# A decoder trunk in fp32: when weights are cast beside the copies and evacuations of a seven-product scheme

## The chip, the cores and the metric

The kernel runs on one core of a Trainium2 chip. The metric is the device time of one execution in microseconds (us); less is better. Engines are named as the profile names them: PE (TensorE, matmuls), PEld (its weight loads), DVE (VectorE), ACT (ScalarE), POOL (GpSimd, here mostly the issuer of accumulating DMAs) and SP (SyncE, the issuer of loads).

## What is computed

Two layers on a sequence of 512 tokens with 1024 features, everything in float32. Each layer adds half a SwiGLU feed-forward (FFN), a mixer, and half a second FFN; the mixer of layer 0 is a gated linear attention, that of layer 1 a stick-breaking attention. A final RMSNorm ends it. The FFN has 2816 inner columns:

```python
def swiglu(h, w_gate, w_up, w_down):
    return (jax.nn.silu(h @ w_gate) * (h @ w_up)) @ w_down
...
for i in range(DEPTH):          # DEPTH = 2
    x = x + 0.5 * swiglu(rmsnorm(x, ffn1_norm[i]), ffn1_w_gate[i], ffn1_w_up[i], ffn1_w_down[i])
    h = rmsnorm(x, mix_norm[i])
    y = gla_mixer(h, ...) if i % 2 == 0 else sb_mixer(h, ...)
    x = x + y
    x = x + 0.5 * swiglu(rmsnorm(x, ffn2_norm[i]), ffn2_w_gate[i], ffn2_w_up[i], ffn2_w_down[i])
return rmsnorm(x, final_norm)
```

So there are four FFNs, and the change concerns them alone.

## The kernel before

**Products.** Activations lie transposed, features on the 128 partitions, the 512 tokens along the row (T = 512, H = 256 is half of them). A float32 product is made of three fast ones: each weight tile is split into a high part, which ACT casts (`wh`, line 138 in `Entry.split`), and a low part, raw minus high, which DVE subtracts (`wl`, line 139). Activations are split in the same way (`hh`, `hl`, lines 816 and 817). Each logical matmul is then wh·h, wl·h and wh·l, so PE's order of work always needs two other engines a little ahead of it.

**Seven products for eight.** Lines 694 to 799 (`seven`) compute a chunk of 256 weight columns in a scheme of seven half-size products in place of eight. Beside the raw weights it needs sums of weight quarters, which DVE makes: `s12` (L704, L705) and `s34` (L710, L711), the "second sums". One chunk is two entries of the feed. The first, `body_1`, has three weight units (a11 of 128x512, s12 of 128x1024, a2 of 128x1024) and four products, in this order: into ps_w with a11; into ps_q with s12; again into ps_w with s12; into ps_z with a2. Between the first and the third ACT copies ps_w to ps_z (L746), since both sums begin with that product; the third adds to ps_w and so must wait for the copy. The second entry, `body_2`, has one unit (s34) and three products: into ps_w, ps_q, ps_w. Results are evacuated by ACT copies and silus and by DVE adds and gates (L729, L732, L765, L769), then closed, that is split into hh and hl. An FFN has 18 such chunks (9 gate, 9 up); the others go by plain products (`feat`).

**Down projection.** Six groups of one or two chunks (`GROUPS`) are projected back as soon as their activations are closed. Groups 1 and 3 go by the same scheme (`seven_down`, lines 354 to 450), in two parts each, so 4 pairs in each FFN and 16 in all. Here `body_1` makes two products b11 (one for each of two 128-column halves m = 0, 1) into ws[0] and ws[1], copies both to zs (L408), then makes t1 into ps_q, t2 on to ws and b21, with the first half of a2, on to zs; behind them come the DVE adds of ps_q, ps_w and ps_z into the residual x (`add`, L396). `body_2` makes t3 on to ws (so it needs s34's split and the add of ws done), b22 on to ps_q, and t4 on to ws with the second half of a2. The other groups' products are evacuated by DVE into x (L345) or, for the products named in `HOMES`, by ACT into a scratch tile that POOL adds to x with an accumulating DMA (L340, L341): one in each part of groups 0 and 2, three in each part of group 4.

**Feed.** `Feed.start` (lines 146 to 161) opens the next entry. Before that it splits, that is casts, this entry and up to two behind it, as long as their big units (128x1024) are not more than four, the number of buffers. Loads of raw weights are issued up to six entries ahead on SP's queue. Instructions go to each engine in an order that a scheduler makes from the order of the program and priorities; on the engine they then run in that order.

Of the kernel before, what the change touches and what calls it, by code (L numbers as in the profile page):

```python
# [10 lines left out]
F32 = mybir.dt.float32  # L11
F32R = mybir.dt.float32r
# [3 lines left out]
ALU = mybir.AluOpType  # L16
PSUM = bass.MemoryType.PSUM

P = 128
T = 512  # L20
# [26 lines left out]
def decoder(ctx: ExitStack, tc: tile.TileContext, a: dict, out: bass.AP):  # L47
    nc = tc.nc
# [5 lines left out]
    wp = ctx.enter_context(tc.tile_pool(name="wp", bufs=4))  # L54
# [53 lines left out]
    class Entry:  # L108
# [3 lines left out]

        def __init__(self, units, body):
            self.units, self.body, self.W, self.views = units, body, None, None

        def view(self):

# [1 line left out]
                self.views = [view(ch.load()) for ch, view, _, _ in self.units]  # L119
            return self.views  # L120

        def split(self):
            if self.W is None:
                self.W = []
                for r, (_, _, n, m) in zip(self.view(), self.units):
                    few = n * m < 1024
                    if few:

                        h, l = (
                            st["few"].tile([P, n * m], F32R, tag="v" + t, bufs=1, name="w" + t) for t in "hl"  # L130
                        )
                    else:
                        h, l = (wp.tile([P, n * m], F32R, tag="w" + t, bufs=4, name="w" + t) for t in "hl")
                    h, l = (t.rearrange("p (n m) -> p n m", m=m) for t in (h, l))
                    pieces = r if isinstance(r, tuple) else (r,)
                    for i, part in enumerate(pieces):
                        k = slice(i * n // len(pieces), (i + 1) * n // len(pieces))
                        st["cut"] = nc.scalar.copy(h[:, k], part).ins  # L138
                        nc.vector.tensor_tensor(out=l[:, k], in0=part, in1=h[:, k].bitcast(F32), op=ALU.subtract)  # L139
                    self.W.append((h, l))  # L140

    class Feed:
        def __init__(self):
# [210 lines left out]
    def seven_down(pool, w, r0, hs, part):  # L354
# [3 lines left out]
        H = T // 2  # L358
# [5 lines left out]
        v = {}  # L364
# [31 lines left out]
            nc.vector.scalar_tensor_tensor(out=x, in0=ps, scalar=0.5, in1=x, op0=ALU.mult, op1=ALU.add)  # L396

        def body_1(W):
            a11, s, v["a2"] = W
            ws, zs, qs = [], [], []  # L400
            for m in range(2):
                ws.append(psum("ps_w")[:, 0:H])
                prod(ws[m], a11, 0, m, "b11", True)
            for m in range(2):


                zs.append(psum("ps_z")[:, 0:H])
                nc.scalar.copy(zs[m], ws[m])  # L408
# [74 lines left out]
    st = {}  # L483
# [129 lines left out]
    class FFN:  # L613
# [12 lines left out]
        def __init__(self, wg, wu, wd, gi, nxt, first=False, last=False):  # L626
# [7 lines left out]
            for group, (c0, c1) in enumerate(self.GROUPS):  # L634
# [59 lines left out]
        def seven(self, ch, group=None):  # L694
# [31 lines left out]
            def gate(o, c, t):  # L726

                if group is None:
                    st["silu"] = nc.scalar.activation(pair(o[:, c : c + H]), t, AF.Silu).ins  # L729
                else:  # L730
                    g = self.gates[0 if o is v["o"][0] else 1]
                    nc.vector.tensor_tensor(  # L732
                        out=pair(o[:, c : c + H]), in0=t, in1=pair(g[:, c : c + H]), op=ALU.mult
                    )

            def body_1(W):


                a11, s, a2 = W
                v["a2"] = a2  # L740
                v["w"], v["q"] = psum("ps_w"), psum("ps_q")
                z = psum("ps_z")[:, 0:H]
                w, q = (v[n][:, 0:H] for n in "wq")
                o0, o1 = v["o"] = [self.tp.tile([P, T], F32, tag="t", name=n) for n in ("o0", "o1")]
                prod(w, a11, 0, half(0, 0))
                nc.scalar.copy(z, w)  # L746
# [5 lines left out]
                nc.scalar.copy(pair(o0[:, H:T]), flat(w))  # L752
                yield
                prod(z, a2, 0, half(4, 0), first=False)
                gate(o0, 0, flat(z))
                yield

            def body_2(W):
                (s,) = W
                w, q = (v[n][:, 0:H] for n in "wq")  # L760
                o0, o1 = v["o"]
                prod(w, s, 0, lambda j: self.t_half(2, j), first=False)
                u3 = self.tp.tile([P, H], F32, tag="c", bufs=1, name="u3")
                nc.scalar.copy(pair(u3), flat(w))
                nc.vector.tensor_tensor(out=o1[:, H:T], in0=u3, in1=o1[:, H:T], op=ALU.add)  # L765
                yield
                prod(q, s, 4, half(4, 1), first=False)
                oh = pair(o0[:, H:T])
                nc.vector.tensor_tensor(out=oh, in0=flat(q), in1=oh, op=ALU.add)  # L769
                gate(o0, H, oh)  # L770
                if group is not None:
                    close_0(o0)
                gate(o1, H, pair(o1[:, H:T]))
                yield
                prod(w, v["a2"], 0, lambda j: self.t_half(3, j), first=False, c0=P)
                gate(o1, 0, flat(w))
# [83 lines left out]
        def evac_u(self, ps, group):  # L860
            t = self.tp.tile([P, T], F32, tag="t", name="t")
            if not self.normed:
                nc.vector.tensor_tensor(out=pair(t), in0=flat(ps), in1=pair(st["R"]), op=ALU.mult)
            nc.vector.tensor_tensor(
                out=pair(t), in0=flat(ps) if self.normed else pair(t), in1=pair(self.gates.pop(0)), op=ALU.mult
            )
            self.close(t, group)

        def close(self, t, group):
            h = self.hp.tile([P, T], F32R, tag="hh", name="hh")  # L870
# [454 lines left out]
    class SB:  # L1325
# [588 lines left out]
```

## Time and profile before

| | us |
|---|---|
| median of 3 runs | 1779.91 (1779.62 to 1782.33) |
| the profiled execution | 1779.44 |
| its span (first to last instruction) | 1777.5 |
| PE busy in it | 1756.3 |
| DVE busy | 1508.6 |
| ACT busy | 1081.6 |
| mean granted clock of PE | 0.999 of full speed |

Times in the profile count from the start of the span. A row of a timeline holds the start, the duration, the engine, the line, the operation, the tiles (output, then inputs) and their shapes; two equal instructions in a row are one row with x2. A duration on ACT or DVE is longer than the distance to the next instruction, since neighbours overlap. A bracket at the end of a row is the idle time ahead of the instruction and what ended it. A row of the waits holds who waited for whom, the total, the number of times and the longest wait.

### The profile page before, as it was taken

The page shows a single profiled execution, that of the slowest core. Times are in us where ns is not written, and L with a number is a line of the kernel's source. Part 1 is how long each engine was busy: PE and PEld are TensorE (multiplying, and loading weights), DVE is VectorE, ACT ScalarE, POOL GpSimd, SP SyncE. Part 2 cuts the span into 40 slices and gives each one's busy share as a digit, 9 for nine tenths or more (in the row PEclk, how much of TensorE's full clock was granted, in tenths as well). Part 3 has the DMA queues.
Part 4 walks back from the last instruction along what each step waited for, and adds up shares of the span by engine and source line. Part 5 has one row for each costly group of instructions (what it writes and reads, how often), then busy time and mean ns, then how long its engine had stood idle before and what let it go on. Part 6 is the DMA issues. An engine that isn't in the chain of part 4 may idle for free.

```text
span 1777.5 us, 31388 instructions
## 1 busy us (share of the span) xinstructions
PE 1756.3 (99%) x12714; PEld 1630.4 (92%) x12714; DVE 1508.6 (85%) x2471; ACT 1081.6 (61%) x1886; POOL 58.4 (3%) x80
## 2 busy tenths in 40 slices
PE   9999999999999999999999999999999999999998
PEld 8999999889888899999889999999888888999997
DVE  8999797786888989888798988967898679997985
ACT  7556556554655556555565555555889745665655
POOL 0000000200000000000000000010000000000000
PEclk9999999999999999999999999999999999999999
DMA  5543435422123433344424344342212134434342
GB/s 168 153 120 118 125 103 148 112 72 72 49 95 95 130 108 119 119 119 126 141 85 130 103 124 135 110 120 83 84 49 78 66 95 131 131 108 129 114 131 65
DMA packets 186820, 193.93 MB, mean 109 GB/s; under 512 B 4978, under 2 KB 171172, under 8 KB 186676
## 3 DMA queue, kind: packets, MB, share of 16 engines
q1 hardware_dynamic: 177760, 175.91, 31.7%
q0 software_dynamic: 8672, 15.74, 4.9%
q8 instruction: 99, 1.62, 0.4%
q14 instruction: 45, 0.37, 0.1%
q10 hardware_dynamic: 244, 0.29, 0.0%
HBM read 175.17 MB, written 2.10 MB: 100 GB/s over the span
## 4 chain that ended last, share of the span: by engine, by line
PE 67%; DVE 22%; ACT 5%; DMA 3%; issue 3%; POOL 0%; DVEq 0%; SPq 0%; ACTq 0%; POOLq 0%
PE ps_w L719 16%; PE ps_d L80 11%; PE ps_q L719 8%; PE ps_f L80 7%; DVE wl L139 5%; PE ps_t L80 4%; PE ps_z L719 4%; PE ps_w L390 4%; PE ps_b L80 3%; PE ps_q L390 2%; ACT wh L138 2%; DMA raw<-in_ffn_w_gate_dram 1%; DVE ts L826 1%; PE ps_z L1402 1%; DVE nl L817 1%
## 5 line engine op out<-in xcount | busy, mean ns | idle before, releaser
L139 DVE TENSOR_TENSOR wl<-raw,wh 128x1024 fp32r<-128x1024 f32 x241 | 255.0, 1059 | 59.8 <-ACT wh L138 59.1
L138 ACT CAST wh<-raw 128x1024 fp32r<-128x1024 f32 x241 | 221.7, 921 | 77.1 <-PE ps_f L80 22.6
L139 DVE TENSOR_TENSOR wl<-s,wh 128x1024 fp32r<-128x1024 f32 x176 | 214.3, 1218 | 47.2 <-ACT wh L138 47.2
L719 PE MATMUL ps_w<-th,wh 128*128 128x256 f32 x864 | 239.4, 277 | 4.2 <-ACT ps_z L746 4.1
L719 PE MATMUL ps_w<-th,wl 128*128 128x256 f32 x864 | 237.6, 275 | 0.0
L719 PE MATMUL ps_w<-tl,wh 128*128 128x256 f32 x864 | 237.6, 275 | 0.0
L138 ACT CAST wh<-s 128x1024 fp32r<-128x1024 f32 x176 | 184.1, 1046 | 69.1 <-DVE s L705 19.3
L719 PEld LDWEIGHTS ps_w<-th,wh 128*128 128x128 f32 x864 | 165.8, 192 | 7.6 <-ACT ps_z L746 7.6
L80 PE MATMUL ps_f<-xh,wh 128*128 128x512 f32 x432 | 166.4, 386 | 0.0
L719 PEld LDWEIGHTS ps_w<-tl,wh 128*128 128x128 f32 x864 | 165.9, 192 | 0.0
L719 PEld LDWEIGHTS ps_w<-th,wl 128*128 128x128 f32 x864 | 165.8, 192 | 0.0
L80 PE MATMUL ps_f<-xh,wl 128*128 128x512 f32 x432 | 164.2, 380 | 0.5 <-DVE wl L139 0.5
L80 PE MATMUL ps_f<-xl,wh 128*128 128x512 f32 x432 | 163.9, 379 | 0.0
L80 PE MATMUL ps_d<-hl,wh 128*128 128x512 f32 x416 | 158.0, 380 | 1.7 <-DVE hl L817 1.7
L80 PE MATMUL ps_d<-hh,wh 128*128 128x512 f32 x416 | 158.0, 380 | 0.5 <-ACT hh L816 0.5
L80 PE MATMUL ps_d<-hh,wl 128*128 128x512 f32 x416 | 157.7, 379 | 0.0
L139 DVE TENSOR_TENSOR wl<-rawd,wh 128x1024 fp32r<-128x1024 f32 (+1 forms) x100 | 96.0, 963 | 16.0 <-ACT wh L138 15.8
L138 ACT CAST wh<-rawd 128x1024 fp32r<-128x1024 f32 (+1 forms) x100 | 82.8, 845 | 39.3 <-PE ps_d L80 25.6
L341 POOL DMA_DIRECT2D x<-d x56 | 48.6, 879 | 1531.1 <-ACT d L340 829.9
L80 PEld LDWEIGHTS ps_f<-xl,wh 128*128 128x128 f32 x432 | 81.6, 189 | 11.5
L80 PEld LDWEIGHTS ps_f<-xh,wl 128*128 128x128 f32 x432 | 81.7, 189 | 11.3 <-DVE wl L139 0.9
L80 PEld LDWEIGHTS ps_f<-xh,wh 128*128 128x128 f32 x432 | 81.7, 189 | 10.8
(355 smaller groups left out, 5324.9 us busy)
## 6 DMA issues: line engine op xcount, KB each, us to landing
raw<-in_ffn_w_gate_dram SPq DMA_DIRECT2D x43, 1024.0 KB, 5.5
raw<-in_ffn_w_up_dram SPq DMA_DIRECT2D x43, 1024.0 KB, 5.4
rawd<-in_ffn_w_down_dram SPq DMA_DIRECT2D x84, 512.0 KB, 3.7
x<-d POOLq DMA_DIRECT2D x56, 256.0 KB, 4.6
raw<-in_gla_w_in_dram SPq DMA_DIRECT2D x12, 1024.0 KB, 5.3
raw<-in_sb_w_in_dram SPq DMA_DIRECT2D x16, 512.0 KB, 3.8
raw<-in_gla_w_out_dram SPq DMA_DIRECT2D x4, 1024.0 KB, 5.0
raw<-in_sb_w_in_dram SPq DMA_DIRECT2D x4, 1024.0 KB, 5.2
```

The lines of the kernel that those rows point to most:

```text
L80: st["pe"] = nc.tensor.matmul(ps, l, r, start=first, stop=last).ins
L138: st["cut"] = nc.scalar.copy(h[:, k], part).ins
L139: nc.vector.tensor_tensor(out=l[:, k], in0=part, in1=h[:, k].bitcast(F32), op=ALU.subtract)
L341: nc.gpsimd.dma_start(xs[k], d, accum_op=ALU.add)
L390: st["pe"] = nc.tensor.matmul(ps, l_, r_, start=first and c + n == 0, stop=c == 1 and n == 2, skip_group_check=True).ins
L719: st["pe"] = nc.tensor.matmul(o, l_, r_, start=first and j + n == 0, stop=j == 3 and n == 2, skip_group_check=True).ins
L817: nc.vector.tensor_tensor(out=l, in0=t, in1=h.bitcast(F32), op=ALU.subtract)
L826: nc.vector.tensor_tensor(out=o, in0=p, in1=q, op=ALU.subtract)
L1402: nc.tensor.matmul(o_, l_, r_, start=first, stop=last, skip_group_check=True)
```

## The change

Four things are altered.

1. The z copies, evacuations, gates and closes of the seven entries are issued with high priority (`ahead()`).
2. The second sums (s34) of a seven entry are cast only behind that entry's copy of ps_w to ps_z: `body_1` calls `split` for the second entry itself and gives the copy as the instruction behind which ACT's casts are issued. `Feed.start` stops its look-ahead at a second entry whose copy isn't there yet.
3. In a down half the unit a2 is held: its split is made in `body_1` behind the z copies (`settle`), and right behind it the split of the down half's own second sums. `Feed.start` doesn't look further than an entry with a held unit that isn't yet split.
4. In the last FFN, the second part of group 4 is evacuated by DVE alone (no `HOMES`), so three ACT evacuations and three accumulating DMAs become three DVE adds.

The matmuls, PE's order and SP's loads stay as they are.

```diff
-        def split(self):
+        def split(self, after=None):
             if self.W is None:
                 self.W = []
...
+                for i, (r, (_, _, n, m)) in enumerate(zip(self.view(), self.units)):
+                    if i == self.held:
+                        self.W.append(None)
+                        continue
+                    self.W.append(self.parts(r, n, m, after))
+
+        def settle(self, after):
+            i = self.held
+            _, _, n, m = self.units[i]
+            self.W[i] = self.parts(self.view()[i], n, m, after)
+            return self.W[i]
+
+        def parts(self, r, n, m, after):
...
+            pieces = r if isinstance(r, tuple) else (r,)
+            for i, part in enumerate(pieces):
+                k = slice(i * n // len(pieces), (i + 1) * n // len(pieces))
+                with tc.issue_after(after) if after is not None else ExitStack():
+                    nc.scalar.copy(h[:, k], part)
+                nc.vector.tensor_tensor(out=l[:, k], in0=part, in1=h[:, k].bitcast(F32), op=ALU.subtract)
+            return h, l
...
-            for e in self.q[i : i + 3]:
+            for n, e in enumerate(self.q[i : i + 3]):
+                if e.v is not None and "copied" not in e.v and self.q[i + n - 2].second:
+                    break
                 used += sum(n * m >= 1024 for _, _, n, m in e.units)
                 if used > 4:
                     break
                 e.split()
+                if e.held is not None and e.W[e.held] is None:
+                    break
...
+    def ahead():
+
+        return tc.high_priority(4000)
```

In `seven_down`:

```diff
         def body_1(W):
-            a11, s, v["a2"] = W
+            a11, s = W[0:2]
...
-                nc.scalar.copy(zs[m], ws[m])
+                with ahead():
+                    copied = nc.scalar.copy(zs[m], ws[m]).ins
+            v["a2"] = v["first"].settle(copied)
+            v["last"].split()
             yield
...
+        feed.q[-1].held = 2
+        v["first"] = feed.q[-1]
...
+        feed.q[-1].second = True
+        v["last"] = feed.q[-1]
```

In `FFN`, the list of down parts and `seven`:

```diff
-                    (wd, c0 * 256, n, self.hs[group], part, nxt if end else None, 0, homes) for part in range(n)
+                    (
...
+                        () if last and group == 4 and part else homes,
+                    )
+                    for part in range(n)
...
                 prod(w, a11, 0, half(0, 0))
-                nc.scalar.copy(z, w)
+                with ahead():
+                    v["copied"] = nc.scalar.copy(z, w).ins
+                v["second"].split(v["copied"])
                 yield
                 prod(q, s, 0, lambda j: self.t_half(0, j))
-                nc.scalar.copy(pair(o1[:, H:T]), flat(q))
+                with ahead():
+                    nc.scalar.copy(pair(o1[:, H:T]), flat(q))
...
+            v["second"] = feed.q[-1]
+            feed.q[-1].second, feed.q[-1].v = True, v
```

The same `with ahead():` is put around the other evacuations and gates of the seven entries and around the gate and close of the plain up products.

More of the change, by code (lines that the diff above doesn't have):

```diff
@@ L114, in __init__ @@
             self.units, self.body, self.W, self.views = units, body, None, None
+            self.second, self.v, self.held = False, None, None
         def view(self):
@@ L681, in __init__ @@
                 downs = [
-                    (wd, c0 * 256, n, self.hs[group], part, nxt if end else None, 0, homes) for part in range(n)
+                    (
+                        wd,
+                        c0 * 256,
+                        n,
+                        self.hs[group],
+                        part,
+                        nxt if end else None,
+                        0,
+                        () if last and group == 4 and part else homes,
+                    )
+                    for part in range(n)
                 ]
@@ L745, in body_1 @@
                 prod(w, a11, 0, half(0, 0))
-                nc.scalar.copy(z, w)
+                with ahead():
+                    v["copied"] = nc.scalar.copy(z, w).ins
+                v["second"].split(v["copied"])
                 yield
                 prod(q, s, 0, lambda j: self.t_half(0, j))
-                nc.scalar.copy(pair(o1[:, H:T]), flat(q))
+                with ahead():
+                    nc.scalar.copy(pair(o1[:, H:T]), flat(q))
                 yield
                 prod(w, s, 4, lambda j: self.t_half(1, j), first=False)
-                nc.scalar.copy(pair(o0[:, H:T]), flat(w))
+                with ahead():
+                    nc.scalar.copy(pair(o0[:, H:T]), flat(w))
                 yield
                 prod(z, a2, 0, half(4, 0), first=False)
-                gate(o0, 0, flat(z))
+                with ahead():
+                    gate(o0, 0, flat(z))
                 yield
@@ L763, in body_2 @@
                 u3 = self.tp.tile([P, H], F32, tag="c", bufs=1, name="u3")
-                nc.scalar.copy(pair(u3), flat(w))
-                nc.vector.tensor_tensor(out=o1[:, H:T], in0=u3, in1=o1[:, H:T], op=ALU.add)
+                with ahead():
+                    nc.scalar.copy(pair(u3), flat(w))
+                    nc.vector.tensor_tensor(out=o1[:, H:T], in0=u3, in1=o1[:, H:T], op=ALU.add)
                 yield
@@ L768, in body_2 @@
                 oh = pair(o0[:, H:T])
-                nc.vector.tensor_tensor(out=oh, in0=flat(q), in1=oh, op=ALU.add)
-                gate(o0, H, oh)
+                with ahead():
+                    nc.vector.tensor_tensor(out=oh, in0=flat(q), in1=oh, op=ALU.add)
+                    gate(o0, H, oh)
                 if group is not None:
                     close_0(o0)
-                gate(o1, H, pair(o1[:, H:T]))
+                with ahead():
+                    gate(o1, H, pair(o1[:, H:T]))
                 yield
                 prod(w, v["a2"], 0, lambda j: self.t_half(3, j), first=False, c0=P)
-                gate(o1, 0, flat(w))
+                with ahead():
+                    gate(o1, 0, flat(w))
                 if group is not None:
@@ L863, in evac_u @@
                 nc.vector.tensor_tensor(out=pair(t), in0=flat(ps), in1=pair(st["R"]), op=ALU.mult)
[L864 to L867, printed above, removed]
+            with ahead():
+                nc.vector.tensor_tensor(
+                    out=pair(t), in0=flat(ps) if self.normed else pair(t), in1=pair(self.gates.pop(0)), op=ALU.mult
+                )
+                self.close(t, group)
         def close(self, t, group):
```

22 lines of the change are left out of this document (7 added, 15 removed).

## The prediction

> **What bounds the kernel now.** I read the page first: the span, the busy shares, the chain that ended last.
>
> ```profile
> span 1777.5 us, 31388 instructions
> ...
> PE 1756.3 (99%) x12714; PEld 1630.4 (92%) x12714; DVE 1508.6 (85%) x2471; ACT 1081.6 (61%) x1886; POOL 58.4 (3%) x80
> ...
> PE 67%; DVE 22%; ACT 5%; DMA 3%; issue 3%; POOL 0%; DVEq 0%; SPq 0%; ACTq 0%; POOLq 0%
> ```
>
> PE sets the end: 1756.3 of 1777.5 us, and its products are not touched by the change. So the time can move only through what PE waits for, and all that is to be had from waits is a share of the 1777.5 − 1756.3 = 21.2 us (more by what modelled ends hide). But DVE is at 85% over the whole span, so work put ahead of something urgent on DVE is paid for. The Trainium skill, "Perfetto Trace Analysis", section "Identifying the Most-Contended Engine", warns that a busy share of matmuls says little, since pipelined ones overlap; the trace agrees (matmuls of 0.28 us start every 0.11 us below), and I count waits from start to start.
>
> Second, the waits of PE by what ended them. The columns are total, times, longest, in us:
>
> ```profile
> PE ps_w L719 <- ACT ps_z L746: 4.1, 10, 1.2
> PE ps_d L80 <- DVE hl L817: 1.7, 2, 0.8
> PE ps_T L1570 <- DMA x<-d: 1.6, 2, 0.8
> ```
>
> The first and third are the waits at which the change aims; the second it leaves alone.
>
> **Term 1, the z copies.** In a seven entry PE's third product goes on adding to ps_w, so it needs ACT's copy z<-w (L746). The timelines of ACT and PE at the first such wait:
>
> ```profile
> 76.03 1.03 ACT L138 CAST wh<-s 128x1024 fp32r<-128x1024 f32 x1
> 76.96 0.36 ACT L746 COPY ps_z<-ps_w 128x256 f32<-128x256 f32 x1
> ```
> ```profile
> 76.12 0.28 PE L719 MATMUL ps_q<-tl,wh 128*128 128x256 f32 x1
> 77.38 0.38 PE L719 MATMUL ps_w<-th,wh 128*128 128x256 f32 x1 [0.99 <-ACT ps_z L746]
> 77.59 0.28 PE L719 MATMUL ps_w<-th,wl 128*128 128x256 f32 x1
> ```
> ```profile
> 124.30 1.04 ACT L138 CAST wh<-s 128x1024 fp32r<-128x1024 f32 x1
> 125.24 0.37 ACT L746 COPY ps_z<-ps_w 128x256 f32<-128x256 f32 x1
> ```
>
> ACT is casting the second sums of the entry when ps_w is ready, and the copy starts 0.94 later. PE's q product ends its issue at 76.12, the next would go at 76.23, and it goes at 77.38: 1.15 late; the matmul behind it follows after 0.21 instead of 0.11, another 0.10. The view counts 4.1 in 10 waits; counted from start to start over all 72 third products, 18 are late, by 7.1 in sum (the pipelined ends hide 0.16 in each counted wait, and eight waits whole). With 18 × 0.10 the ceiling is 8.9. The change issues this cast behind the copy. Then the copy starts when ps_w is ready: the second one at about 124.2 rather than 125.24, well before PE's need. Where the copy now stands behind hh or ts casts of 128x512 instead (once each in the first FFN of each layer) I leave 0.35, an estimate of under one such cast of 0.53 (below): 0.7. **Net −8.2.** The moved cast is needed only by the entry's second half, three products (3 × 1.34 = 4.02) after the first one's last matmul; until ACT reads ps_w 0.31, the copy 0.31 (76.96 to the next cast), the cast 0.95 and the subtract 1.14 leave 1.3 of that, so these products hide it. Without that cover each of 72 entries could cost what is missing, which is why I keep a rival for it.
>
> **Term 2, the end of the last FFN.** POOL, DVE and PE there:
>
> ```profile
> 1742.12 0.88 POOL L341 DMA_DIRECT2D x<-d  x1 [21.21 <-ACT hh L816]
> 1743.97 1.74 POOL L341 DMA_DIRECT2D x<-d  x2 [0.97 <-ACT d L340]
> ```
> ```profile
> 1744.40 0.69 DVE L345 SCALAR_TENSOR_TENSOR x<-ps_d,x 128x512 f32<-128x512 f32 x1 [1.55 <-PE ps_d L80]
> ```
> ```profile
> 1744.20 2.35 PE L1570 MATMUL ps_T<-ident,x 128*128 128x128 f32 x20
> 1747.38 0.66 PE L1570 MATMUL ps_T<-ident,x 128*128 128x128 f32 x4 [0.84 <-DMA x<-d]
> 1748.84 1.09 PE L1570 MATMUL ps_T<-ident,x 128*128 128x128 f32 x8 [0.81 <-DMA x<-d]
> ```
>
> The transposes wait for the last accumulating DMAs: 0.84 + 0.81, with the ends' 0.16 each 1.97. Three DVE adds of 0.69 take the place of three ACT evacuations and three DMAs. DVE was idle for 1.55 just ahead, so the adds end by about 1745.1, ahead of the transposes that had to wait. Bounds: 0 if DVE falls behind there (three adds are 2.07, the idle 1.55), −2.0 if they fit. I take **−1.9**, since the first of the three tiles can be added while DVE idles. On POOL three issues go, and the load of the last norm's gain (fin) comes to stand behind an accumulate that waits for ACT; DVE meets its wait for fin early in the last group, with weights behind it that are not yet due, so I cost it at nothing; without that slack it is one wait of 1 to 2 us, as long as those of the accumulates above.
>
> **Term 3, the down halves.** In the 16 seven_down pairs (4 in each FFN) the last weights (a2, two pieces of 128x512) and the down's second sums (128x1024) are now cast behind the z copies. ACT, then DVE, at the first of them before the change:
>
> ```profile
> 133.18 1.04 ACT L138 CAST wh<-s 128x1024 fp32r<-128x1024 f32 x1
> 134.13 0.63 ACT L408 COPY ps_z<-ps_w 128x256 f32<-128x256 f32 x2
> 134.69 0.62 ACT L138 CAST wh<-raw 128x512 fp32r<-128x512 f32 x1
> 135.22 0.61 ACT L816 CAST hh<-o 128x512 fp32r<-128x512 f32 x1
> ```
> ```profile
> 132.54 1.22 DVE L139 TENSOR_TENSOR wl<-s,wh 128x1024 fp32r<-128x1024 f32 x1
> 133.67 0.68 DVE L817 TENSOR_TENSOR hl<-o,hh 128x512 fp32r<-128x512 f32 x1
> 134.28 0.42 DVE L732 TENSOR_TENSOR o<-ps_w,o 128x256 f32<-128x256 f32 x1
> 134.61 1.21 DVE L139 TENSOR_TENSOR wl<-s,wh 128x1024 fp32r<-128x1024 f32 x1
> 135.86 0.69 DVE L817 TENSOR_TENSOR hl<-o,hh 128x512 fp32r<-128x512 f32 x1
> 136.47 0.74 DVE L396 SCALAR_TENSOR_TENSOR x<-ps_q,x 128x256 f32<-128x256 f32 x2
> 137.14 0.74 DVE L396 SCALAR_TENSOR_TENSOR x<-ps_w,x 128x256 f32<-128x256 f32 x2
> 137.80 0.68 DVE L139 TENSOR_TENSOR wl<-raw,wh 128x512 fp32r<-128x512 f32 x1
> ```
>
> Here are the steps' prices, start to start: a cast of 512 takes 0.53, of 1024 0.95, a z copy 0.28, a subtract of 1024 1.13, of 512 0.61, an add of 256 0.33 (0.41 to its end). PE's first product of the second entry, t3, adds on to ps_w, so it must wait for the add x<-ps_w of the first half (L396). Before, the adds stood on DVE directly behind hl. In the changed program's DVE order stand ahead of that add: the two subtracts of a2, one add x<-ps_q, the subtract of the second sums, and the other x<-ps_q. The subtract waits for its cast, which is the last of three behind the z copies. That PE does wait for this add is in the trace of before, at the one place in the first FFN where DVE was late:
>
> ```profile
> 281.09 0.75 DVE L396 SCALAR_TENSOR_TENSOR x<-ps_w,x 128x256 f32<-128x256 f32 x2
> ```
> ```profile
> 281.41 0.28 PE L390 MATMUL ps_z<-hl,wh 128*128 128x256 f32 x1
> 281.56 0.38 PE L390 MATMUL ps_w<-nh,wh 128*128 128x256 f32 x1
> ```
> ```profile
>   DVE x L396: 0.7, 3
> ```
>
> The add of m = 0 ends at 281.09 + 0.41 = 281.50, and t3 starts at 281.56. The last row is what PE sat idle for at L390.
>
> The lower bound of the new stall, counted from the start of the last b11 matmul: 0.31 until ACT reads ps_w (a product's reader starts about that long after its last matmul), last z copy 0.28, casts 2 × 0.53 + 1.04, 0.04 to DVE, subtract 1.13, x<-ps_q 0.33, x<-ps_w 0.41, 0.06 to PE: 4.66. PE meanwhile issues t1, t2 and b21, each 12 matmuls of 0.112 = 1.34, so it wants t3 at 0.11 + 4.02 = 4.13. So at least 0.53 is missing even when both engines are punctual, and 0.10 is lost behind it: 16 × 0.63 = 10.1.
>
> The upper bound: DVE has no idle in the rows from 132.54 on, and the add of m = 0 ends at 137.55. Into that stretch go the two subtracts of 0.61, so it ends at about 138.77 and t3 starts at 138.83, where before it went at 137.86:
>
> ```profile
> L390 PE MATMUL ps_q<-hh,wh x128: 275/275/275, 133.8 to 1713.4; 128*128 128x256 f32 x128
> L390 PE MATMUL ps_w<-t,wh x128: 275/275/275, 138.2 to 1715.0; 128*128 128x256 f32 x128
> ```
>
> (t1 starts at 133.8; the t operand is t3's fourth matmul, so t3 began 0.34 ahead of 138.2.) That is 0.95 and the 0.10: 16 × 1.05 = 16.8. DVE is ahead of this stretch by the subtracts that left it, but the gate and hh casts behind it hold DVE up. For three of four places I take 0.92, for one, where DVE has air, 0.58: 3.34 + 4 × 0.10 = 3.74 an FFN. **Net +15.0.** The waits for this add that were there already lie inside this: the 0.7 shown, 1.4 from start to start. **−1.4.**
>
> The Trainium skill, "Perfetto Trace Analysis", section "Per-engine timelines", says that DVE and ACT take instructions strictly in order, and only PE may pull weight loads forward. By that rule the add cannot pass the waiting subtract, and the sum is the one made here; without it term 3 would vanish and the time would be that of rival 1. The trace agrees as far as it goes: at 134.61 to 137.14 DVE starts in the order of the program.
>
> **Sum.** 1779.44 (the profiled execution: span 1777.5 and 1.94 around it) − 8.2 − 1.9 − 1.4 + 15.0 = 1782.9. The median of the runs shown is 1779.91, 0.47 above that execution, so I predict 1783.4.
>
> Two further new waits I cost at nothing: the a2 subtracts come 1.0 us or more ahead of b21 (cast pieces end 1.65 after the last b11 matmul, b21 is due at 2.79), and the priority of gates and closes alters DVE's order only among work that PE needs later. If that cover were gone, a 0.3 to 0.6 late piece would cost as much at each of 16, 5 to 10 us: rival 2.
>
> **Rivals.**
>
> *1. The down halves are no loss: faster.* One mechanism: the add of the first half arrives within 4.13 us of the last b11 matmul, because the casts behind the z copies run earlier than I let them (ACT is at 61%) or DVE meets the subtract with its cast long done. From that point on term 3 is 0, and the rest stays: 1779.91 − 8.2 − 1.9 − 1.4 = 1768.4. A partial form decides the sign: under 11.5 / 16 = 0.72 a place the change is a gain, under 0.50 it is one that can be told. For it: ACT's idle. Against it: the minimal chain is 0.53 too long with no queue at all, and the lowest sum with it, at 10.1, gives 1778.5.
>
> *2. The copies are freed, but DVE falls behind.* With gates, copies and closes pulled forward, and the second sums' casts later, the subtracts that PE needs next are late by the same amounts. For it: DVE's 85%, and its rows above without idle. Against it: the subtract of the second sums has 1.3 us to spare. Then term 1 is about 0 and term 3 is whole: 1779.91 − 1.9 + 13.6 = 1791.6; with half of term 1, 1787.5.
>
> *3. Nothing is changed that counts.* If the stalls at t3 let ACT and DVE catch up so that only one or two of four places show them in full and the rest only the bound (term 3 of 10 to 12), gains and losses cancel: 1778.4 to 1780.4. It is the lower edge of my account with a reason of its own (less work queued on both engines after each stall), and ends as no change.
>
> **How the numbers follow.** 0.2% is 3.6 us, about what a measurement of this kernel can tell from no change: faster is under 1776.3, slower above 1783.5. My own account with its bounds (1778.5 to 1785.2 for term 3 of 10.1 to 16.8) gets 0.60, rival 3 is 0.13 beside it, rival 2 0.17, rival 1 0.10. Of my account, half lies above 1783.5, the other half within. So slower is 0.30 + 0.17 = 0.47, same 0.30 + 0.13 = 0.43, faster 0.10. The range leaves out rival 1 and the upper end of rival 2: 1777.5 to 1789.
>
> **What would show it.** In the changed profile: the wait of PE ps_w for ACT ps_z at the seven entries falls from 4.1 to under 0.5; the wait of PE ps_T for DMA x<-d is gone; PE's wait at the down halves for DVE x rises from 0.7 in 3 to some 7 to 13 in up to 16, with PE's t3 starting 0.06 after the add of the first half, and that add directly behind the subtract of the second sums. I am wrong if PE's t3 starts 0.11 after the matmul ahead of it (rival 1), or if new waits for wl or for s stand at the seven entries (rival 2).

## The result, and the profile after

The change makes the kernel slower: 1789.66 us median of 6 runs (1789.08 to 1791.54) against 1780.38 for the kernel before on the same chip, a ratio of 1.0055 with a 95% interval of 1.0045 to 1.0065. Against the 1779.91 of the table ahead of the prediction that is 9.75 more, where 3.5 were predicted, and it lies 0.7 above the end of the range. The profiled execution took 1789.55.

The page of the changed kernel:

```profile
span 1787.6 us, 31349 instructions
...
PE 1757.8 (98%) x12714; PEld 1632.0 (91%) x12714; DVE 1508.1 (84%) x2474; ACT 1072.5 (60%) x1883; POOL 55.7 (3%) x77
...
PE 70%; DVE 19%; ACT 7%; issue 3%; DMA 2%; DVEq 0%; ACTq 0%; SPq 0%
```

PE is busy for 1.5 us more and the span is 10.1 longer: nearly all of it is waiting. The waits of PE by what ended them (total, times, longest):

```profile
PE ps_w L412 <- DVE x L418: 12.8, 16, 0.9
PE ps_w L412 <- ACT u L460: 2.1, 5, 0.5
...
PE ps_w L758 <- ACT ps_z L786: 0.2, 1, 0.2
```

Lines have moved: L412 and L418 are L390 and L396 of before, L460 is L435, L758 and L786 are L719 and L746, L152 and L153 the casts and subtracts (L138 and L139 of before). Three of the forecast's steps can be read off at once: the wait for the z copies fell from 4.1 to 0.2, the wait of ps_T for x<-d is not in the view any more, and the wait for the adds at the down halves went from 0.7 in 3 to 12.8 in 16. The second row was not in the forecast.

The first down half, on ACT, DVE and PE:

```profile
132.13 1.14 ACT L866 CAST hh<-o 128x512 fp32r<-128x512 f32 x2 [2.64 <-DVE o L771]
133.18 0.64 ACT L431 COPY ps_z<-ps_w 128x256 f32<-128x256 f32 x2
133.74 1.14 ACT L152 CAST wh<-rawd 128x512 fp32r<-128x512 f32 x2
134.78 1.07 ACT L152 CAST wh<-s 128x1024 fp32r<-128x1024 f32 x1
```
```profile
135.60 0.42 DVE L418 SCALAR_TENSOR_TENSOR x<-ps_q,x 128x256 f32<-128x256 f32 x1
135.94 1.22 DVE L153 TENSOR_TENSOR wl<-s,wh 128x1024 fp32r<-128x1024 f32 x1
137.07 0.42 DVE L418 SCALAR_TENSOR_TENSOR x<-ps_q,x 128x256 f32<-128x256 f32 x1
137.40 0.75 DVE L418 SCALAR_TENSOR_TENSOR x<-ps_w,x 128x256 f32<-128x256 f32 x2
```
```profile
136.80 0.28 PE L412 MATMUL ps_z<-hl,wh 128*128 128x256 f32 x1
137.96 0.35 PE L412 MATMUL ps_w<-nh,wh 128*128 128x256 f32 x1 [0.89 <-DVE x L418]
```

Here stands the chain of the forecast: three casts behind the z copies, the subtract behind the last of them, the adds of ps_q and then of ps_w behind the subtract, and PE's t3 1.05 later than it was due (136.91). Note also that ACT idled for 2.64 just before the hh casts: the casts that come too late here had room there.

The second parts show the wait that was not foreseen. ACT in the same FFN:

```profile
177.25 1.05 ACT L152 CAST wh<-rawd 128x1024 fp32r<-128x1024 f32 x1 [2.49 <-DMA rawd<-in_ffn_w_down_dram]
178.20 1.04 ACT L152 CAST wh<-s 128x1024 fp32r<-128x1024 f32 x1
179.14 0.64 ACT L460 COPY u<-ps_w 128x256 f32<-128x256 f32 x2
```
```profile
179.01 0.28 PE L412 MATMUL ps_q<-hl,wh 128*128 128x256 f32 x1
179.56 0.38 PE L412 MATMUL ps_w<-nh,wh 128*128 128x256 f32 x1 [0.28 <-ACT u L460]
179.77 0.28 PE L412 MATMUL ps_w<-nh,wl 128*128 128x256 f32 x1
```

ACT waits 2.49 for a load of down weights; behind that cast stand another one and the copies of ps_w to u, and PE's t4 adds to the ps_w that they read. SP's timeline tells why the load is late, before and after:

```profile
167.16 7.14 SPq L105 DMA_DIRECT2D rawd<-in_ffn_w_down_dram  x3
```
```profile
173.51 0.97 SPq L105 DMA_DIRECT2D rawd<-in_ffn_w_down_dram  x2
```

And DVE after:

```profile
172.79 1.30 DVE L153 TENSOR_TENSOR wl<-rawd,wh 128x512 fp32r<-128x512 f32 x2 [2.46 <-ACT wh L152]
```

The load goes out as soon as a raw tile of the down weights is free (there are two). It was given back after a2's subtract, at 167.16; now a2 is held until after the z copies, the first of its two subtracts runs from 172.79 to about 173.48, and the load goes at 173.51, 6.3 later, although its place in SP's queue is the same. Over the kernel, ACT's waits for such loads grew sevenfold, before and after:

```profile
ACT wh L138 <- DMA rawd<-in_ffn_w_down_dram: 3.9, 8, 0.8
```
```profile
ACT wh L152 <- DMA rawd<-in_ffn_w_down_dram: 27.7, 14, 2.7
```

Counted from start to start of PE's matmuls, as in the prediction, lateness grew by 9.9 in the whole trace:

| place | before | after | difference |
|---|---|---|---|
| third product of the seven entries, and the matmul behind it | 8.9 | 0.7 | −8.2 |
| first product of their second entries, and the matmul behind it | 0.0 | 1.1 | +1.1 |
| transposes at the end | 2.1 | 0.0 | −2.1 |
| t3 of the down halves | 0.7 | 15.5 | +14.8 |
| t4, behind the copies to u | 0.0 | 3.5 | +3.5 |
| the second matmul of t3 and t4 | 0.6 | 2.0 | +1.4 |
| all else | 22.0 | 21.4 | −0.6 |

The second row is new and too small for the view of the waits. It is another product that adds on to a ps_w that ACT copies out first: at 79.02, where it is latest, it starts 0.12 late, 0.05 behind the end of ACT's copy o<-ps_w.

### The profile page after: what moved, and what is told of

The parts are those of the page before. It is cut to its first block, busy times and chain, and to the rows that moved or that the text cites. A ratio compares the mean times of both kernels' runs of the same rounds, so it can differ in the third digit from the quotient of the medians.

```text
span 1787.6 us, 31349 instructions
## 1 busy us (share of the span) xinstructions
PE 1757.8 (98%) x12714; PEld 1632.0 (91%) x12714; DVE 1508.1 (84%) x2474; ACT 1072.5 (60%) x1883; POOL 55.7 (3%) x77
## 4 chain that ended last, share of the span: by engine, by line
PE 70%; DVE 19%; ACT 7%; issue 3%; DMA 2%; DVEq 0%; ACTq 0%; SPq 0%
PE ps_w L758 18%; PE ps_d L80 13%; PE ps_f L80 9%; PE ps_q L758 9%; DVE wl L153 5%; PE ps_t L80 4%; PE ps_z L758 4%; PE ps_b L80 3%; PE ps_w L412 3%; ACT wh L152 2%; PE ps_z L1453 1%; PE ps_oT L1538 1%; DMA rawd<-in_ffn_w_down_dram 1%; DVE ts L876 1%; PE ps_bt L80 1%
## 5 line engine op out<-in xcount | busy, mean ns | idle before, releaser
L153 DVE TENSOR_TENSOR wl<-raw,wh 128x1024 fp32r<-128x1024 f32 x241 | 255.4, 1061 | 47.1 <-ACT wh L152 46.3
L153 DVE TENSOR_TENSOR wl<-s,wh 128x1024 fp32r<-128x1024 f32 x176 | 214.8, 1220 | 76.3 <-ACT wh L152 75.2
L152 ACT CAST wh<-raw 128x1024 fp32r<-128x1024 f32 x241 | 221.9, 921 | 63.3 <-PE ps_f L80 21.9
L758 PE MATMUL ps_w<-th,wh 128*128 128x256 f32 x864 | 238.9, 276 | 0.2 <-ACT ps_z L786 0.2
L758 PE MATMUL ps_w<-th,wl 128*128 128x256 f32 x864 | 237.6, 275 | 0.0
L758 PE MATMUL ps_w<-tl,wh 128*128 128x256 f32 x864 | 237.6, 275 | 0.0
L152 ACT CAST wh<-s 128x1024 fp32r<-128x1024 f32 x176 | 185.4, 1053 | 35.9 <-DVE s L744 17.6
L758 PEld LDWEIGHTS ps_w<-th,wh 128*128 128x128 f32 x864 | 165.8, 192 | 0.9 <-ACT ps_z L786 0.4
L758 PEld LDWEIGHTS ps_w<-tl,wh 128*128 128x128 f32 x864 | 165.9, 192 | 0.0
L758 PEld LDWEIGHTS ps_w<-th,wl 128*128 128x128 f32 x864 | 165.9, 192 | 0.0
L153 DVE TENSOR_TENSOR wl<-rawd,wh 128x1024 fp32r<-128x1024 f32 (+1 forms) x100 | 95.2, 965 | 30.4 <-ACT wh L152 30.2
L152 ACT CAST wh<-rawd 128x1024 fp32r<-128x1024 f32 (+1 forms) x100 | 82.8, 845 | 60.2 <-DMA rawd<-in_ffn_w_down_dram 27.7
L80 PEld LDWEIGHTS ps_f<-xl,wh 128*128 128x128 f32 x432 | 81.6, 189 | 11.5
```

The costliest lines, as they stand in the source:

```text
L80: st["pe"] = nc.tensor.matmul(ps, l, r, start=first, stop=last).ins
L758: st["pe"] = nc.tensor.matmul(o, l_, r_, start=first and j + n == 0, stop=j == 3 and n == 2, skip_group_check=True).ins
```

## The experiments

Two theories stood at the start. A: the loss lies in the two waits of the down halves, and without them the rest of the change gains some 9 us. B: ACT and DVE are too full around the down halves, and every order of the casts gives another wait. Ratios below are to the kernel before, with 95% intervals.

**Without the down part.** Edit to the changed kernel:

```diff
-            a11, s = W[0:2]
+            a11, s, v["a2"] = W
...
-            v["a2"] = v["first"].settle(copied)
-            v["last"].split()
...
-        feed.q[-1].held = 2
```

> The changed kernel with the down halves as before: a2 and the down's second sums are again cast by the feed's look-ahead, ahead of the z copies. Theory A (the loss lies in two waits of the down halves, 19.7 us of start-to-start lateness of PE in the changed kernel's trace, and the rest of the change gains what the trace shows, 6.8 + 0.5 at the third products and 2.1 at the end): 9 to 10 us under the kernel before, ratio 0.9945 to 0.995; waits of PE ps_w for DVE x 0.7 or less, for ACT u none. Theory B (DVE is full, and what the copies gain comes back at other waits; the down halves only show it): within 2 us of before.

Measured: 1779.88, ratio 1.0003 (0.9994 to 1.0012). The number is B's. The waits of PE:

```profile
PE ps_w L412 <- ACT ps_z L431: 4.0, 7, 0.8
PE ps_R L80 <- ACT sh L590: 2.5, 3, 1.2
PE ps_w L755 <- DVE wl L153: 2.2, 4, 1.3
```

Adds and copies to u are no longer waited for, as A had it, and third products and transposes keep their gain (−7.6 and −2.1 from start to start). But the z copies of the down halves themselves are now late, 6.2 from start to start with the matmul behind. ACT at a second part:

```profile
172.44 1.04 ACT L152 CAST wh<-rawd 128x1024 fp32r<-128x1024 f32 x1 [0.48 <-DMA rawd<-in_ffn_w_down_dram]
173.39 0.64 ACT L431 COPY ps_z<-ps_w 128x256 f32<-128x256 f32 x2
```

A cast of the entry after the next, itself waiting for its load, stands ahead of the copies. So the down part was not mere loss: it also kept the look-ahead from putting such casts there. The third row, for wl, is rival 2's wait at four seven entries: PE waits there for the subtract of the second sums. At two of them (147.1 and 1021.4) DVE stood idle for 1.11 and 2.06 before it, for a load of gate weights. This profiled execution took 1782.24, 2.4 above the median of the run, so not all of these waits need be in the others.

**Which of the held casts does it.** First only a2 stays behind the copies (the down's second sums are split at the head of `body_1`):

```diff
             a11, s = W[0:2]
+            v["last"].split()
...
             v["a2"] = v["first"].settle(copied)
-            v["last"].split()
```

> The changed kernel, but the down's second sums are split at the head of the down half's first entry, ahead of the z copies; only a2 stays behind them. Theory A, first wait (the add that t3 needs is queued behind the subtract of the second sums, whose cast is the last of three behind the copies): with one of the three gone from there the wait of PE ps_w for DVE x falls from 12.8 to under 2. Theory A, second wait (the raw tile of the down weights is given back only after a2's subtract, so a later load lands late, and ACT's cast of it holds up the copies to u): this stays, the wait for ACT u 2 or more, since a2 still keeps the raw tile. Time about 4 to 5 us under before. Rival C (each piece behind the copies costs alike, by its own length on ACT): of t3's 15.7 half stays, and the time is 0 to 3 us above before.

Measured: 1792.03, ratio 1.0074 (1.0058 to 1.0089).

```profile
PE ps_w L412 <- ACT u L460: 11.9, 8, 1.9
...
PE ps_z L412 <- DVE wl L153: 1.5, 6, 0.3
```

The wait for the adds is gone from the view (2.3 of its 15.5 are left from start to start), so most of it did come from the third cast; but the time is not the expected one. The late load is as late as before, and PE, no longer held up at t3, now meets it in full: 11.9 at the 8 second parts. In the changed kernel the two waits overlapped, and the 2.1 shown there was what t3's wait left of the other. The last row is new: at 6 places b21 waits for a2's subtract, which the prediction had costed at nothing. ACT's wait at the same place grew from 2.49 to 3.50:

```profile
176.97 1.05 ACT L152 CAST wh<-rawd 128x1024 fp32r<-128x1024 f32 x1 [3.50 <-DMA rawd<-in_ffn_w_down_dram]
```

Then the other half, only the second sums behind the copies:

```diff
-            a11, s = W[0:2]
+            a11, s, v["a2"] = W
...
-            v["a2"] = v["first"].settle(copied)
-            v["last"].split()
+            v["last"].late = False
+            v["last"].split(copied)
...
-        feed.q[-1].held = 2
+        v["last"].late = True
```

with `if e.late: break` in `Feed.start`.

> The other half of it: a2 is cast by the look-ahead as before, only the down's second sums are cast behind the z copies. Theory A: the raw tile is free early again, so the wait of PE ps_w for ACT u is gone; the chain to the add is 0.31 + 0.28 + 1.04 + 0.04 + 1.13 + 0.33 + 0.33 + 0.41 + 0.06 = 3.93 against 4.13, so t3 waits little (0 to 0.3 at each of 16). Time 5 to 10 us under before. Rival C: half of t3's 15.7 stays, about 2 us under before. Rival D (the copies to u wait for the number of casts ahead of them on ACT, not for a load): the wait for ACT u stays at about 2.

Measured: 1776.06, ratio 0.9982 (0.9973 to 0.9991).

```profile
PE ps_w L415 <- ACT wh L153: 2.8, 10, 0.3
...
PE ps_w L415 <- DVE x L421: 0.5, 2, 0.3
```
```profile
ACT wh L153 <- DMA rawd<-in_ffn_w_down_dram: 7.3, 6, 2.8
```

With a2's raw tile free early, ACT's waits for the loads of down weights fall from 27.7 to 7.3 and the wait for the copies to u is gone, though the cast of the loaded tile and the next entry's still stand ahead of them: without the load's lateness they cost nothing. t3 waits 0.42 to 0.45 at 12 of 16 places, where 0 to 0.3 were expected, and 5.3 in all; the gain is 3.6 where 5 to 10 were expected. The first of the 12, on DVE and PE:

```profile
138.41 0.75 DVE L421 SCALAR_TENSOR_TENSOR x<-ps_w,x 128x256 f32<-128x256 f32 x2
```
```profile
138.97 0.35 PE L415 MATMUL ps_w<-nh,wh 128*128 128x256 f32 x1 [0.29 <-ACT wh L153]
```

The view names a cast on ACT for ten of these waits, but that cast is one of a later entry's and only ends within 0.02 of t3's start. What fits all 12 is the add: t3 starts 0.145 to 0.147 behind the end of the first add of ps_w, as in the changed kernel. Here the chain begins late: ACT's second z copy stands behind an hh cast and starts at 135.21, about 0.5 after ps_w could be read. The profiled execution took 1778.83, 2.8 above the median of the run; it has a third product 1.4 late behind a load of gate weights, so the z copies' gain was smaller in it.

**Is it the place on DVE's queue alone?** The subtract of the second sums is put behind the first add of ps_w, with all three casts where the change has them:

```diff
-            v["last"].split()
+            v["last"].split(sub=False)
...
                 prod(ws[m], s, 2, m, "t2", False)
-                add(m, 0, 1, flat(ws[m]))
+                with tc.issue_after(st["low"]) if m else ahead():
+                    add(m, 0, 1, flat(ws[m]))
+                if m == 0:
+                    st["low"] = v["last"].lower(st["added"])
```

(`lower` issues the subtract behind the instruction it is given.)

> The changed kernel with all three casts behind the z copies, but on DVE the subtract of the down's second sums is put behind the first add of ps_w instead of in front of it. Theory A: t3's first matmul no longer waits (PE ps_w for DVE x under 2 in place of 12.8); its second may wait up to 0.3 for the subtract; the wait for ACT u stays. Time about 12 to 15 us under the changed kernel, 2 to 5 under before. Theory B or a wait of t3 for the subtract or its cast themselves: the wait only moves to t3's second matmul, with 0.5 or more at each place, and the time stays within 4 us of the changed kernel.

Measured: 1788.55, ratio 1.0052 (1.0038 to 1.0066): the rival's. PE at the first place:

```profile
136.83 0.28 PE L419 MATMUL ps_w<-nh,wh 128*128 128x256 f32 x1
137.79 0.38 PE L419 MATMUL ps_w<-nh,wl 128*128 128x256 f32 x1 [0.68 <-DVE wl L161]
```

t3's first matmul is on time, its second waits for the subtract itself (0.47 or 0.85 late at each of the 16). DVE there:

```profile
134.31 1.30 DVE L161 TENSOR_TENSOR wl<-rawd,wh 128x512 fp32r<-128x512 f32 x2 [0.31 <-ACT wh L152]
...
136.52 1.22 DVE L161 TENSOR_TENSOR wl<-s,wh 128x1024 fp32r<-128x1024 f32 x1
```

From the first a2 cast on, DVE works without a pause: two subtracts, three adds, the third subtract, to 137.74. PE needs that subtract's result at 136.94, and the stretch can't begin before the casts behind the z copies. So between these two orders the one on DVE sets which wait is seen, and the time does not differ; what has to go is work from this stretch.

**The copies to u.** They get priority over the cast of the next entry that stands ahead of them on ACT:

```diff
-                nc.scalar.copy(pair(u3[:, m]), flat(ws[m]))
+                with ahead():
+                    nc.scalar.copy(pair(u3[:, m]), flat(ws[m]))
```

> The changed kernel, but the copies to u in the down halves' second entry go ahead of the following casts on ACT, except the cast that waits for the late load. Theory A2: they start about 0.95 earlier where they were late, so the wait of PE ps_w for ACT u (2.1) falls under 0.5, the wait for DVE x stays at 12 to 13, and the time is 3 to 4.5 us under the changed kernel. Rival (the copies wait for the load alone): the wait for ACT u stays, and the time is the changed kernel's.

Measured: 1785.37, ratio 1.0031 (1.0020 to 1.0042), 4.3 under the changed kernel.

```profile
PE ps_w L412 <- DVE x L418: 13.0, 16, 1.0
```

No row for ACT u is left. The overlooked wait was worth 4.3 of the 9.75. ACT still waits for the loads (29.1 in 16 waits), so PE's wait for these copies took both: the late load, and one more cast behind it.

**The down part alone on the kernel before.** The changed kernel with `ahead()` empty, without the split behind the copy of ps_w and its rule in `Feed.start`, and with group 4 as before:

```diff
-        return tc.high_priority(4000)
+        return ExitStack()
...
-                v["second"].split(v["copied"])
```

> The kernel before with the down part alone: a2 and the down's second sums behind the z copies, no priority, no second sums of seven entries behind their copies, the last group 4 part as before. Theory A2: the waits of PE ps_w for DVE x (12 to 13) and for ACT u (2 to 4) are there in full, and the third products still wait for ACT ps_z: 15 to 20 us above before (ratio 1.008 to 1.011). Theory E (the down part is what lets the copies of the seven entries gain, and its cost comes from their casts standing ahead of it): under half of that.

Measured: 1796.05, ratio 1.0090 (1.0074 to 1.0105), 16.1 above before.

```profile
PE ps_w L410 <- DVE x L416: 8.4, 16, 0.6
PE ps_w L410 <- ACT u L458: 4.3, 8, 1.2
PE ps_w L756 <- ACT ps_z L784: 3.2, 10, 1.0
PE ps_T L1618 <- DMA x<-d: 2.8, 2, 2.0
```

All four waits stand side by side, as expected, but the one for the adds is 8.4, not 12 to 13: t3 is late by 0.68 to 0.73 from start to start at every place. Together with the first experiment this shows how much the parts lean on each other: by the ratios the other three edits are worth some 6 us on top of the down part (1.0090 to 1.0055) and nothing without it (1.0003).

**The fourth edit alone.**

```diff
-                    (wd, c0 * 256, n, self.hs[group], part, nxt if end else None, 0, homes) for part in range(n)
+                    (wd, c0 * 256, n, self.hs[group], part, nxt if end else None, 0, () if last and group == 4 and part else homes)
+                    for part in range(n)
```

> The kernel before with the fourth edit alone: group 4's second part in the last FFN evacuated by DVE. Theory: the wait of PE ps_T for DMA x<-d (1.6, 1.97 from start to start) is gone and nothing takes its place: 1.5 to 2.1 us under before. Rival: DVE's subtracts in the last group are late by the 2 us of the three adds, or by its wait for the load of fin, and nothing is gained.

Measured: 1778.32, ratio 0.9991 (0.9982 to 0.9999), 1.65 under before; PE's wait for x<-d has gone from the view and nothing has taken its place there.

**Can the gain be kept?** a2 and the second sums are cast by the look-ahead, into ACT's idle 2.6; behind the z copies goes the next entry instead:

```diff
-                e.split()
+                if n == 2 and self.q[i + 1].z == "open":
+                    break
+                e.split(self.q[i].z)
...
-            v["a2"] = v["first"].settle(copied)
-            v["last"].split()
+            v["last"].z = copied
```

> The changed kernel with another rule for the down halves: a2 and the down's second sums are cast by the look-ahead, into the 2.6 us in which ACT idles before the halves in the changed kernel; what is cast behind the z copies is the next entry (s12 of the next seven entry, or the raw tile of a plain down entry), which in the run without the down part stood ahead of them and made PE wait 4.0 for ACT ps_z. Theory A2 (a down half loses whatever of these casts is on the wrong side of its z copies; the rest of the change gains its 9 us only if both waits are gone): waits of PE ps_w for ACT ps_z, ACT u, DVE x and ACT wh at the down halves together under 1.5, time 5 to 7 us under the kernel before (ratio 0.996 to 0.997). Theory B (DVE and ACT together are too full in these stretches, and each order gives another wait): within 2 us of before, with the lateness at another wait of the same size.

Measured: 1781.83, ratio 1.0010 (1.0001 to 1.0019), B's number again.

```profile
PE ps_w L414 <- DVE x L420: 5.7, 13, 0.5
```

At the down halves z copies, copies to u and loads make PE wait no more. But now the subtract of the next s12 stands on DVE between the two adds of ps_w:

```profile
137.10 0.43 DVE L420 SCALAR_TENSOR_TENSOR x<-ps_w,x 128x256 f32<-128x256 f32 x1
137.43 1.23 DVE L153 TENSOR_TENSOR wl<-s,wh 128x1024 fp32r<-128x1024 f32 x1
138.56 0.43 DVE L420 SCALAR_TENSOR_TENSOR x<-ps_w,x 128x256 f32<-128x256 f32 x1
```

From start to start t3's second half is late by 0.69 behind its add at 9 places (the expectation of the next run says 11) and by 0.31 at a tenth. Here, unlike where the down's own subtract was moved, the subtract isn't needed by t3, so here the order on DVE is what is wrong. Last edit, on top of this one: the next entry's subtracts behind the last add of ps_w.

```diff
-                e.split(self.q[i].z)
+                e.split(self.q[i].z, self.q[i].added)
...
-                nc.vector.tensor_tensor(out=l[:, k], in0=part, in1=h[:, k].bitcast(F32), op=ALU.subtract)
+                with tc.issue_after(added) if added is not None else ExitStack():
+                    nc.vector.tensor_tensor(out=l[:, k], in0=part, in1=h[:, k].bitcast(F32), op=ALU.subtract)
```

> The version with the next entry's casts behind the z copies, and now also its DVE subtracts behind the last add of ps_w in the down half (there t3's second half waited 0.69 at 11 places for an add queued behind the subtract of the next s12, the same mechanism as in the changed kernel with another subtract). Theory A2: PE's wait for DVE x (5.7 in 13) falls under 1.5, nothing of the size takes its place, and the gains of the rest stand: 6 to 9 us under the kernel before (ratio 0.995 to 0.9965). Theory B (DVE and ACT are too full there, each order only names another wait): within 2 us of the version without this, that is 1 to 3 above before, with the lateness now at the next entry's subtracts (wl).

Measured: 1774.90, ratio 0.9976 (0.9967 to 0.9985): 4.7 under before and, by the ratios, 14 under the change.

```profile
span 1772.3 us, 31331 instructions
...
PE 1756.7 (99%) x12714; PEld 1631.2 (92%) x12714; DVE 1503.7 (85%) x2474; ACT 1074.8 (61%) x1883; POOL 55.6 (3%) x77
```

Among the waits of PE none of the down halves is left, and 0.2 for ps_z. From start to start the third products and the end have gained 10.1, and 4.9 went back: 3.1 at t3 (its halves are 0.11 to 0.29 late, at 9 places each) and 1.6 at the first products of the second entries. So the expected 6 to 9 was too much, and B is right in part: something came back, as it said. But not every order gives the whole of it back: with DVE as busy as before within 5 us, this one keeps half of the gain.

## Why the prediction was too low

**Direction and mechanism held, the sum did not.** By its own terms, from start to start:

| term | predicted | measured |
|---|---|---|
| 1, z copies | −8.2 | −8.2 |
| 2, end of the last FFN | −1.9 | −2.1 |
| 3, t3 behind the adds, less what was there | +13.6 | +15.4 |
| copies to u, t4 | 0 | +4.3 |
| first products of the second entries | 0 | +1.1 |

(Of the 1.4 in the row of second matmuls above 0.6 goes to t3, 0.8 to t4. All else gave −0.6.)

**The step that failed** is the sentence "Two further new waits I cost at nothing", and the "Two": a third wait, for the copies to u, was put at nothing by not being seen, and it took 4.3. The sentence looked at what is behind the held casts on ACT and DVE, not at what they give back. Holding a2 holds the raw tile, the tile holds SP's next load, the load holds a cast on ACT, and behind that cast stand copies that PE needs. In the text of the change nothing of SP's moves, and in its order nothing does; its times do. The priority run prices this at 4.3, and the pair a2 held / second sums held shows its cause: the wait for the copies goes where a2 is cast early, and it grows to 11.9 where only a2 is held. The direct test, a third raw tile with a2 held, was not run.

**Term 3** was sized between its bounds of 10.1 and 16.8 at 13.6 net and came out at 15.4 net; three places in four wait 1.06 from start to start where 0.92 was taken, the fourth 0.68 where it was 0.58. Most of that is the last link: t3 started 0.145 behind the add, not 0.06, which makes 16 × 0.085 = 1.4. Without it three places in four stand at the prediction's upper bound, which is 138.83 − 137.86 = 0.97 (it wrote 0.95). The chain itself was right, as far as a2's two pieces belong to it: a2 held without the second sums, or the second sums without a2, each does away with most of the wait for the add. What was wrong in it is the weight put on DVE's order ("the add cannot pass the waiting subtract"): with the add ahead of the subtract PE waits for the subtract, and the two intervals overlap. The Trainium skill's rule on strict order, "Perfetto Trace Analysis", section "Per-engine timelines", agrees with the DVE rows shown here, but rival 1 was not the alternative to it, as the prediction had it: with the subtract moved behind the add, the work behind the late casts still held t3 up.

**Term 1** came out as forecast, but the seven entries lost 1.1 elsewhere: the first products of the second entries wait a little, which the forecast did not have. (Of the closes, the change gives priority only to those of the plain up products; those of the seven entries stand outside `ahead()`, other than the list of the change says.) **Term 2** held, and alone it is worth 1.65 (the interval allows 0.2 to 3.2).

**Rival 2** named nearly the measured time (1787.5 to 1791.6) by another mechanism, so its nearness is luck: term 1 held, and no wait for the seven entries' subtracts is in the view of the changed kernel. They do appear in the run without the down part (2.2 in 4). **Rival 1** fell, but so did what it took for granted, that the rest gains 11.5 once the casts behind the z copies cost nothing: without the down part the z copies of the down halves are late instead, and the time is that of before. The forecast added up terms that share ACT's queue as if each would stay when another is taken away. Part of the gain was kept by two orders, the second sums alone behind the copies (3.6) and the last experiment (4.7); their intervals overlap.

## What to carry to other kernels

When a step is moved to later, follow what it frees as well as what it feeds: its input tile, the load that waits for that tile, and everything queued behind the first reader of the load. A queue has room or not at a place, not on average: ACT was 60% busy, idled 2.6 us before the first down half and still made PE wait behind it; what stands ahead of an urgent copy should be the casts that are due soonest, and no others. Waits of one chain overlap, so a wait's share in the trace is no price for removing it; take it out and look at which one is next.

## What was not expected of the hardware

At the down halves PE's start behind its releaser takes one of two values. At all 16 places of the changed kernel t3 starts 0.145 to 0.147 behind the end of the add (at the first, 137.40 + 0.41 = 137.81 and 137.96), and PEld loads its weights 0.03 ahead of the matmul. Before the change, where t3 had to wait at all, it was 0.054 to 0.055, with the load at most 0.002 ahead. The length of the wait does not decide it: with the next entry behind the z copies, t3's second half starts 0.054 behind its add after PE sat idle for 0.53, and with a2 alone held, 0.053 behind a copy to u after 1.85. The long value was found at t3 alone, in the four kernels (the change, the second sums alone late, the copies to u first, the down part alone) in which the second sums are cast behind the z copies and the add stands behind their subtract. What makes the difference was not tried.
